# Routing the gathered tokens first, seven places for gathered rows, and one-hot products moved out of PSUM in runs of four tokens

## The chip, the cores and the metric

One Trainium2 chip, one core. The metric is the device time of one execution in microseconds; the median of the runs counts.

## The reference

Two transformer layers over 512 tokens of width 1024, all in float32. Everything of interest is in the last step of the second layer, an expert layer with 16384 experts of one row each:

```python
q = (xn @ wq).reshape(bsz, s, 8, 2, 128)
sub = jnp.einsum('bshpd,hpnd->bshpn', q, subkeys)        # 16 score rows of 128 per token
s_top, i_top = lax.top_k(sub, 16)
cand = s_top[..., 0, :, None] + s_top[..., 1, None, :]   # 16 x 16 per head
best, pos = lax.top_k(cand, 16)
expert = take_along_axis(i_top0 * 128 + i_top1, pos)     # 8 heads x 16 experts per token
gate = softmax(best)
a = gelu(einsum('td,ted->te', x, u_tab[expert]))
y = einsum('te,ted->td', gate * a, v_tab[expert])
```

## The kernel before

**How the experts are computed.** The 512 tokens are four blocks of 128 (tb 0 to 3). For the first 320 tokens (N_U: blocks 0 and 1 and half of block 2) the products with the rows of `u` are made densely: `u_block` takes 128 experts, loads a unit of 512 KB (`raw`, four buffers), splits it in two float32r parts (`whi` by ScalarE, L137, and `wlo` by VectorE, L139), and makes 24 matmuls of 320 columns (three passes times eight), then a gelu. For the first 384 tokens the products with `v` are dense too: `v_block` loads and splits 128 rows of `v` and makes 18 matmuls of 512 columns into six banks that live to the end. The weights between the two come from the routing: `build` makes a matrix of 128 x 128 experts for each token as a product of two one-hot matrices on TensorE (L1048), moves four tokens at a time out of PSUM (ScalarE, L1049), and writes most of it to `g_dram`, some to `gres`.

For the other 192 tokens rows are **gathered**: a gather (L881, an indirect DMA issued by GpSimd) brings one row of 4 KB for each of 128 partitions, 512 KB in all, into one of GBUFS = 4 places, and one VectorE instruction consumes it. There are 64 for the second half of block 2 (`ga2`, L889; two tokens' worth on the two halves of the partitions), then 128 with `u` for block 3 (L897), then 128 with `v` for block 3 (L904, into `h[3]`). A place is free again once VectorE has consumed it.

**Stages.** First 16 projections for the scores, then a *first stage* of 100 `u_block`s whose results go to `a_dram` (the pairs in SPAIR), in which the routing is done alongside; then a *second stage* over 64 pairs of blocks: two `v_block`s for each pair, and for the pairs not in SPAIR also two `u_block`s.

**What sets the order.** Work alongside is written as generators: `route` (`top_keys`, `keys`, `build`) and `gat` (the gathers). Each `yield` gives an assumed number of microseconds, and `advance(gen, us)` lets a generator go on until the allowance is used; a `yield 0.0` ends the call. In the first stage each `u_block` allows R_US = 2.1 for `route` and, once block 2's experts are known (`ready`), G1_US = 0.9 for `gat`, of which a gather takes 1.2; in the second stage each `v_block` allows G_US = 2.4, two gathers. `routed` runs `top_keys` of all blocks, then `keys` 2 and 3, `keys` and `build` of 0 and 1, then whatever of the 64 gathers of block 2 is left in one go (`while not made2: next(gat)`), `weights2`, and `build` of 2. On every engine instructions run in their order; the sequence within that is made by the tile scheduler.

Of the kernel before, what the change touches and what calls it, by code (L numbers as in the profile page):

```python
# [9 lines left out]
F32 = mybir.dt.float32  # L10
# [12 lines left out]
GBUFS = 4  # L23

R_US = 2.1
TOP_US = 4.0
G1_US = 0.9
G_US = 2.4
# [10 lines left out]
N_RES = 2  # L39

# [3 lines left out]
SPILL = [2 * p + j for p in SPAIR for j in range(2)]  # L44
# [15 lines left out]
def tile_layers(ctx: ExitStack, tc: tile.TileContext, A: dict, out: bass.AP):  # L60
# [8 lines left out]
    keep = pool("keep")  # L69
    ring = pool("ring")  # L70
    small = pool("small", bufs=4)
# [778 lines left out]
    gres = []  # L850
# [34 lines left out]
    def gathered():  # L885
        for k in range(64):
            r = gather(A["peer_u"], gidx2, k)
            with tc.issue_after(pace[0]):
                V.scalar_tensor_tensor(r, r, 1.0, hn2, op0=OP.mult, op1=OP.mult, accum_out=ga2[:, k:k + 1])  # L889
            yield 1.2  # L890
        made2.append(True)
        while len(ready) < 2:
            yield 0.0
        for k in range(128):
            r = gather(A["peer_u"], gidx, k)
            with tc.issue_after(pace[0]):
                V.scalar_tensor_tensor(r, r, 1.0, hn3, op0=OP.mult, op1=OP.mult, accum_out=ga[:, k:k + 1])  # L897
            yield 1.2
        S.activation(ga, ga, AF.Gelu_apprx_tanh)
        V.tensor_tensor(ga, ga, ggate, op=OP.mult)  # L900
        for k in range(128):
            r = gather(A["peer_v"], gidx, k)
            with tc.issue_after(pace[0]):
                V.scalar_tensor_tensor(h[3], r, ga[:, k:k + 1], h[3], op0=OP.mult, op1=OP.add)  # L904
            yield 1.2

    def top_keys(sub, tb, hps):
        sv, si = tops[tb]
        for hp in hps:
            x = sub[:, hp, :]  # L910
            with order(pace[0]):
                V.max(out=sv[:, hp, 0:8], in_=x)
                V.max_index(out=si[:, hp, 0:8], in_max=sv[:, hp, 0:8], in_values=x)
                V.match_replace(out=x, in_to_replace=sv[:, hp, 0:8], in_values=x, imm_value=-3.0e38)
                V.max(out=sv[:, hp, 8:16], in_=x)
                V.max_index(out=si[:, hp, 8:16], in_max=sv[:, hp, 8:16], in_values=x)
            yield 1.0

    def keys(pr, tb):
# [15 lines left out]
        for j in range(8):  # L935
# [8 lines left out]
            yield 1.1  # L944
# [18 lines left out]
        for a in range(2):  # L963
            for b0 in range(0, 16, 8):
# [12 lines left out]
                yield 1.2  # L977
# [30 lines left out]
        yield 2.0  # L1008
# [13 lines left out]
    def build(pr, tb):  # L1022

        sT = sTs[tb]
        for ts in range(8):
            gt = pr.tile([128, 128, 16], F32, name="gt", bufs=2)
            for t8 in range(0, 16, 8):
# [15 lines left out]
                for q in range(2):  # L1043
# [15 lines left out]
    with ExitStack() as st:  # L1059
# [20 lines left out]
        sub = [pk.tile([128, 16, 128], F32, name=f"sub{tb}") for tb in range(4)]  # L1080
# [4 lines left out]
        def routed():  # L1085
# [6 lines left out]
            pres = pool("pres", side="right")  # L1092
            gres.extend(pres.tile([128, 24, 8, 16], F32, name=f"gres{g}") for g in range(N_RES))
# [15 lines left out]
        for c4 in range(4):  # L1109
# [25 lines left out]
    with ExitStack() as st:  # L1135
# [45 lines left out]
        for p in range(64):  # L1181
            if p < 63:
# [3 lines left out]
            state["debt"] = advance(gat, state["debt"] + G_US)  # L1186
# [3 lines left out]
            state["debt"] = advance(gat, state["debt"] + G_US)  # L1190
# [139 lines left out]
```

## Time and profile before

| | |
|---|---|
| median of 3 runs | 2220.05 us (2218.74 to 2222.28) |
| the profiled execution | 2223.98 us, span 2222.3 us |
| PE busy | 2082.0 us, 94% of the span |
| VectorE busy | 1583.9 us, 71% |
| ScalarE busy | 863.1 us, 39% |
| gathers | 320, 169.18 MB of 476.47 MB moved |

Reading it: a busy share of TensorE counts matmuls whose ends are modelled, so that 94% is not 94% of what it can do; the pitch between two starts in a full stretch tells more. The clock that was granted to TensorE and the share of the 16 DMA engines stand in the table of stretches. A wait behind an arrow names what ended the idle time before an instruction.

### The profile page before, as it was taken

The numbers are of one execution on the slowest core, as the hardware profiler recorded it, in microseconds if no ns is written. First come the engines' busy times: TensorE is split into PE (matmuls) and PEld (weight loads), VectorE is DVE, ScalarE is ACT, GpSimd is POOL, SyncE is SP. The second block draws the span as 40 slices with busy tenths as digits, with TensorE's granted clock in tenths as the row PEclk, the third lists the DMA queues.
The fourth block names the chain that finished last, engine by engine and source line by source line (L and its number), as shares of the span: only waits on it lengthen the run. The fifth ranks groups of instructions, "written<-read, shape, count | busy, mean of one in ns | idle before, by whom it ended". The sixth has DMA issues, their size and how long they took to land.

```text
span 2222.3 us, 29478 instructions
## 1 busy us (share of the span) xinstructions
PE 2082.0 (94%) x11104; PEld 1767.1 (80%) x11104; DVE 1583.9 (71%) x2880; ACT 863.1 (39%) x1303; POOL 501.1 (23%) x383
## 2 busy tenths in 40 slices
PE   7989999999989999999999998899999899898889
PEld 6737888888777778888999997799787677777777
DVE  6984533332479654569999998887888788778873
ACT  4454422222344433333546765563333233232222
POOL 1000000000001000000031214323555556555550
PEclk9989999999999999999999999899999999999999
DMA  5202333333223213322688999999999999999992
GB/s 190 76 20 76 95 96 100 98 114 95 65 83 100 76 63 101 128 93 77 194 301 291 357 309 338 324 339 373 345 352 351 359 363 370 366 348 363 365 324 95
DMA packets 163281, 476.47 MB, mean 214 GB/s; under 512 B 13865, under 2 KB 57265, under 8 KB 161218
## 3 DMA queue, kind: packets, MB, share of 16 engines
q1 hardware_dynamic: 67104, 259.70, 34.1%
q0 software_dynamic: 46656, 169.18, 20.6%
q10 hardware_dynamic: 49378, 45.71, 6.2%
q8 instruction: 87, 1.43, 0.3%
q14 instruction: 56, 0.46, 0.1%
HBM read 432.18 MB, written 42.09 MB: 213 GB/s over the span
## 4 chain that ended last, share of the span: by engine, by line
PE 40%; issue 25%; DMA 14%; DVE 10%; POOL 9%; ACT 1%; POOLq 0%; DVEq 0%; SPq 0%; ACTq 0%
PE bank_a L155 9%; PE bank_a L156 9%; PE bank_a L157 9%; DMA rows<-in_peer_v_dram,gidx 9%; POOL rows L881 8%; PE bank_b L155 3%; PE bank_b L156 3%; PE bank_b L157 3%; DMA rows<-in_peer_u_dram,gidx 3%; DVE wlo L139 2%; DVE h L904 1%; PE bank_b L1048 1%; DVE rows L889 1%; POOL rstd L163 1%; DMA gl<-g_dram 1%
## 5 line engine op out<-in xcount | busy, mean ns | idle before, releaser
L137 ACT CAST whi<-raw 128x1024 fp32r<-128x1024 f32 (+1 forms) x413 | 432.1, 1047 | 851.1 <-PE bank_a L156 332.7
L139 DVE TENSOR_TENSOR wlo<-raw,whi 128x1024 fp32r<-128x1024 f32 (+1 forms) x413 | 500.4, 1214 | 268.2 <-ACT whi L137 265.9
L155 PE MATMUL bank_a<-xhi,whi 128*128 128x320 f32 (+2 forms) x1600 | 552.8, 346 | 9.4 <-ACT whi L137 8.4
L157 PE MATMUL bank_a<-xhi,wlo 128*128 128x320 f32 (+2 forms) x1600 | 546.9, 342 | 9.6 <-DVE wlo L139 9.6
L156 PE MATMUL bank_a<-xlo,whi 128*128 128x320 f32 (+2 forms) x1600 | 549.8, 344 | 0.6 <-DVE xlo L152 0.6
L881 POOL DMA_INDIRECT rows<-in_peer_u_dram,gidx x192 | 265.9, 1385 | 598.0 <-DVE rows L897 214.0
L155 PEld LDWEIGHTS bank_a<-xhi,whi 128*128 128x128 f32 x1600 | 304.9, 191 | 38.1 <-ACT whi L137 9.2
L157 PEld LDWEIGHTS bank_a<-xhi,wlo 128*128 128x128 f32 x1600 | 305.3, 191 | 36.0 <-DVE wlo L139 10.1
L156 PEld LDWEIGHTS bank_a<-xlo,whi 128*128 128x128 f32 x1600 | 305.8, 191 | 26.9 <-DVE xlo L152 1.6
L155 PE MATMUL bank_a<-whi,wvhi 128*128 128x512 f32 x512 | 209.9, 410 | 46.4 <-ACT wvhi L151 46.4
L881 POOL DMA_INDIRECT rows<-in_peer_v_dram,gidx x128 | 198.9, 1554 | 157.8 <-DVE h L904 136.3
L156 PE MATMUL bank_a<-wlo,wvhi 128*128 128x512 f32 x512 | 208.5, 407 | 3.1 <-DVE wlo L139 3.1
L163 POOL TENSOR_TENSOR rstd<-rstd,neghalf 128x1 f32<-128x1 f32 (+2 forms) x37 | 26.5, 718 | 818.9 <-DVE rstd L162 810.9
L157 PE MATMUL bank_a<-whi,wvlo 128*128 128x512 f32 x512 | 209.1, 408 | 1.5 <-DVE wvlo L152 1.5
L904 DVE SCALAR_TENSOR_TENSOR h<-rows,ga,h 128x1024 f32<-128x1024 f32 x128 | 164.2, 1283 | 60.1 <-DMA rows<-in_peer_v_dram,gidx 59.1
L897 DVE SCALAR_TENSOR_TENSOR rows<-rows,h 128x1024 f32<-128x1024 f32 x128 | 154.8, 1220 | 45.4 <-DMA rows<-in_peer_u_dram,gidx 45.1
L155 PEld LDWEIGHTS bank_a<-whi,wvhi 128*128 128x128 f32 x512 | 101.2, 198 | 70.2 <-ACT wvhi L151 50.7
L157 PEld LDWEIGHTS bank_a<-whi,wvlo 128*128 128x128 f32 x512 | 100.9, 197 | 29.5 <-DVE wvlo L152 8.4
L156 PEld LDWEIGHTS bank_a<-wlo,wvhi 128*128 128x128 f32 x512 | 101.5, 198 | 25.3 <-DVE wlo L139 5.0
L151 ACT CAST wvhi<-gl 128x768 fp32r<-128x768 f32 x56 | 45.6, 831 | 164.8 <-DVE gl L1164 98.1
L1049 ACT ACTIVATE gt<-bank_b 128x512 f32<-128x512 f32 x96 | 96.8, 1119 | 10.8 <-PE bank_b L1048 10.1
L155 PE MATMUL bank_b<-whi,wvhi 128*128 128x512 f32 x256 | 100.7, 393 | 0.0
(391 smaller groups left out, 3364.9 us busy)
## 6 DMA issues: line engine op xcount, KB each, us to landing
raw<-in_wt_dram SPq DMA_DIRECT2D x150, 512.0 KB
raw<-in_ut_dram SPq DMA_DIRECT2D x128, 512.0 KB
raw<-in_peer_v_dram SPq DMA_DIRECT2D x128, 512.0 KB
g_dram<-gt ACTq DMA_DIRECT2D x24, 896.0 KB
gl<-g_dram SPq DMA_DIRECT2D x14, 1536.0 KB
a_dram<-ab ACTq DMA_DIRECT2D x25, 640.0 KB
al<-a_dram SPq DMA_DIRECT2D x25, 640.0 KB
rows<-in_peer_u_dram,gidx POOLq DMA_INDIRECT x192
```

The source lines that it names most:

```text
L137: lead[0] = S.copy(hi[:, :n], raw[:, :n]).ins
L139: pace[0] = V.tensor_tensor(lo[:, :n], raw[:, :n], hi[:, :n].bitcast(F32), op=OP.subtract).ins
L151: a = S.copy(hi, src).ins
L155: T.matmul(o, lh, rh, start=start, stop=False)
L156: T.matmul(o, lh, rl, start=False, stop=False)
L157: T.matmul(o, ll, rh, start=False, stop=stop)
L163: G.tensor_tensor(r, r, neghalf[:, :shape[1]], op=OP.pow)
L881: G.indirect_dma_start(out=r, out_offset=None, in_=table, in_offset=bass.IndirectOffsetOnAxis(ap=idx[:, k:k + 1], axis=0))
L889: V.scalar_tensor_tensor(r, r, 1.0, hn2, op0=OP.mult, op1=OP.mult, accum_out=ga2[:, k:k + 1])
L897: V.scalar_tensor_tensor(r, r, 1.0, hn3, op0=OP.mult, op1=OP.mult, accum_out=ga[:, k:k + 1])
L904: V.scalar_tensor_tensor(h[3], r, ga[:, k:k + 1], h[3], op0=OP.mult, op1=OP.add)
L1049: S.activation(gt[:, :, t8 + 4 * q:t8 + 4 * q + 4].rearrange("p i t -> p t i"), gp, AF.Copy, scale=1.0 if made else 2.0 ** -14)
```

## The change

Six things are changed together.

1. GBUFS goes from 4 to 7. Room for it comes from the descriptor memory of the software DMA queue (`dynamic_dma_scratch_size` set to 4096 bytes a partition) and from `sub[0]` and `sub[1]`, which now lie in the memory of `gres`, allocated earlier for it.
2. Routing order: during the projections only blocks 2 and 3 go through `top_keys`; `keys` 2 and 3 follow; only then `top_keys` of blocks 0 and 1.
3. The assumed times of nearly all steps are others (a step of `top_keys` 1.6 for 1.0, a gather 1.3 for 1.2, a step of `build` 2.7 or 3.4 for 2.4).
4. In the first stage one allowance of 3.6 for each block is shared: 1.0 to the gathers as long as block 2's 64 are not made, then 0.5, and the rest to `route`.
5. In the second stage a `v_block` of a pair in SPAIR allows 2.3, of another pair 3.45.
6. The move out of PSUM writes runs of four tokens: the output is taken as it lies (128 x 4), and the PSUM side is read across.

```diff
-GBUFS = 4
+GBUFS = 7
-R_US = 2.1
-TOP_US = 4.0
-G1_US = 0.9
-G_US = 2.4
+TOP_US = 5.0
+R_US = 3.6
+GATHER = 0.5
+G_US = 2.3
+DMA_SCRATCH = 4096
...
-    gres = []
+    pres = pool("pres", side="right")
+    gres = [pres.tile([128, 24, 8, 16], F32, name=f"gres{g}") for g in range(N_RES)]
...
-                    S.activation(gt[:, :, t8 + 4 * q:t8 + 4 * q + 4].rearrange("p i t -> p t i"), gp, AF.Copy,
+                    S.activation(gt[:, :, t8 + 4 * q:t8 + 4 * q + 4], gp.rearrange("p t i -> p i t"), AF.Copy,
                                  scale=1.0 if made else 2.0 ** -14)
-                yield 2.4
+                yield 3.4 if made else 2.7
...
-        sub = [pk.tile([128, 16, 128], F32, name=f"sub{tb}") for tb in range(4)]
+        sub = [gres[tb].rearrange("p s i t -> p (s i t)")[:, 0:2048].rearrange("p (a n) -> p a n", a=16) if tb < 2 else
+               pk.tile([128, 16, 128], F32, name=f"sub{tb}") for tb in range(4)]
...
             yield from keys(pr, 2)
             yield from keys(pr, 3)
+            for tb in (0, 1):
+                yield from top_keys(sub[tb], tb, range(16))
             for tb in (0, 1):
                 yield from keys(pr, tb)
                 yield from build(pr, tb)
...
-            todo += [top_keys(sub[tb], tb, range(c4 * 4, c4 * 4 + 4)) for tb in (2, 3, 0, 1)]
+            todo += [top_keys(sub[tb], tb, range(c4 * 4, c4 * 4 + 4)) for tb in (2, 3)]
...
-                d1 = advance(route, d1 + R_US)
                 if ready:
-                    d2 = advance(gat, d2 + G1_US)
+                    g1 = GATHER * (2 - len(made2))
+                    d2 = advance(gat, d2 + g1)
+                d1 = advance(route, d1 + R_US - (g1 if ready else 0.0))
...
+            g_us = G_US if p in SPAIR else 1.5 * G_US
...
-            state["debt"] = advance(gat, state["debt"] + G_US)
+            state["debt"] = advance(gat, state["debt"] + g_us)
```

What this moves is best seen on VectorE, which consumes the gathers and makes every `wlo`. In units of 512 KB (counted by `wlo`; the first stage begins behind number 157 and ends behind number 260) the first gather is consumed behind unit 175 before and behind unit 169 now, and 84 gathers stand ahead of unit 261 before, 70 now. Of the 64 steps of `top_keys` 32 stand behind the first stage's beginning before, 48 now.

VectorE around the end of block 2's 64 gathers, before (`rows,ga_6475` is a gather for block 2, `rows,ga` one for block 3, `oh` the one-hot matrices, `wlo` a unit):

```order
L889 SCALAR_TENSOR_TENSOR rows,ga_6475<-rows,h_71 128x1024 x4
L139 TENSOR_TENSOR wlo<-raw,whi 128x1024
L889 SCALAR_TENSOR_TENSOR rows,ga_6475<-rows,h_71 128x1024 x3
L1034 TENSOR_TENSOR oh_12130<-iota_7081,sT_7064 128x1024
L889 SCALAR_TENSOR_TENSOR rows,ga_6475<-rows,h_71 128x1024
L1035 TENSOR_TENSOR oh_12131<-iota_7081,sT_7064 128x1024
L889 SCALAR_TENSOR_TENSOR rows,ga_6475<-rows,h_71 128x1024
L1041 TENSOR_TENSOR ohh<-oh_12131,sT_7064 128x1024
L889 SCALAR_TENSOR_TENSOR rows,ga_6475<-rows,h_71 128x1024 x2
L1041 TENSOR_TENSOR ohl<-oh_12131,sT_7064 128x1024
L889 SCALAR_TENSOR_TENSOR rows,ga_6475<-rows,h_71 128x1024
L139 TENSOR_TENSOR wlo<-raw,whi 128x1024
```

The same place now:

```order
L891 SCALAR_TENSOR_TENSOR rows,ga_6475<-rows,h_71 128x1024
L1037 TENSOR_TENSOR oh_12326<-iota_7086,sT_7068 128x1024
L140 TENSOR_TENSOR wlo<-raw,whi 128x1024
L1036 TENSOR_TENSOR oh_12325<-iota_7086,sT_7068 128x1024
L1043 TENSOR_TENSOR ohh<-oh_12326,sT_7069 128x1024
L1043 TENSOR_TENSOR ohl<-oh_12326,sT_7069 128x1024
L891 SCALAR_TENSOR_TENSOR rows,ga_6475<-rows,h_71 128x1024
L140 TENSOR_TENSOR wlo<-raw,whi 128x1024
L891 SCALAR_TENSOR_TENSOR rows,ga_6475<-rows,h_71 128x1024 x4
L899 SCALAR_TENSOR_TENSOR rows,ga<-rows,h_70 128x1024
```

Before, 18 gathers of block 2 stand between the `wlo` of unit 232 and that of unit 235; now four stand together behind one `wlo`, at unit 243.

VectorE at the end of the program, before (`wvlo` are the split weights, L904 the gathers with `v`, L1200 the final additions):

```order
L904 SCALAR_TENSOR_TENSOR h_73<-rows,ga,h_73 128x1024
L139 TENSOR_TENSOR wlo<-raw,whi 128x1024
L152 TENSOR_TENSOR wvlo<-gl,wvhi 128x24x2x16
L139 TENSOR_TENSOR wlo<-raw,whi 128x1024 x2
L152 TENSOR_TENSOR wvlo<-gl,wvhi 128x24x2x16
L139 TENSOR_TENSOR wlo<-raw,whi 128x1024 x2
L152 TENSOR_TENSOR wvlo<-gl,wvhi 128x24x2x16
L139 TENSOR_TENSOR wlo<-raw,whi 128x1024 x2
L152 TENSOR_TENSOR wvlo<-gl,wvhi 128x24x2x16
L139 TENSOR_TENSOR wlo<-raw,whi 128x1024 x3
L1200 TENSOR_TENSOR h_70<-h_70,bank_a 128x512 x2
```

The same place now:

```order
L140 TENSOR_TENSOR wlo<-raw,whi 128x1024
L906 SCALAR_TENSOR_TENSOR h_73<-rows,ga,h_73 128x1024
L140 TENSOR_TENSOR wlo<-raw,whi 128x1024
L906 SCALAR_TENSOR_TENSOR h_73<-rows,ga,h_73 128x1024 x2
L153 TENSOR_TENSOR wvlo<-gl,wvhi 128x24x2x16
L140 TENSOR_TENSOR wlo<-raw,whi 128x1024
L906 SCALAR_TENSOR_TENSOR h_73<-rows,ga,h_73 128x1024 x2
L140 TENSOR_TENSOR wlo<-raw,whi 128x1024
L906 SCALAR_TENSOR_TENSOR h_73<-rows,ga,h_73 128x1024 x2
L140 TENSOR_TENSOR wlo<-raw,whi 128x1024
L1207 TENSOR_TENSOR h_70<-h_70,bank_a 128x512 x2
```

Before, the last ten units have no gather beside them; now gathers stand between the units up to the last one.

## Rows read from the trace of the kernel before

**Rows 1.** Stretches: microseconds; PE, PEld, DVE, ACT, POOL busy; granted clock; DMA share; GB/s

```profile
960.00:1020.00 60.00, 60.00 (x307) 49.56 (x306) 50.65 (x283) 20.53 (x31) 0.00 (x0) 1.00 0.27 88
1020.00:1210.00 190.00, 179.23 (x1279) 172.46 (x1279) 180.14 (x670) 96.77 (x134) 31.34 (x24) 0.97 0.66 219
1210.00:1350.00 140.00, 139.99 (x1177) 137.21 (x1174) 133.00 (x226) 100.06 (x140) 32.62 (x26) 1.00 0.97 335
1350.00:1420.00 70.00, 48.34 (x346) 45.83 (x345) 56.01 (x92) 30.56 (x44) 29.33 (x24) 0.80 0.94 323
1420.00:1504.00 84.00, 84.00 (x725) 82.71 (x724) 69.84 (x100) 53.64 (x76) 17.76 (x14) 1.00 0.97 336
1504.00:2168.00 664.00, 606.04 (x2758) 506.29 (x2758) 547.77 (x612) 205.00 (x235) 353.75 (x232) 0.95 0.96 357
2168.00:2222.30 54.30, 50.33 (x212) 41.05 (x211) 20.62 (x21) 10.86 (x12) 0.00 (x0) 0.94 0.29 97
```

**Rows 2.** Stretches with line 139 alone (`wlo`): how many units VectorE had begun

```profile
0.00:1020.00 1020.00, 189.06 (x157) 0.99 0.29 93
0.00:1504.00 1504.00, 314.30 (x261) 0.98 0.47 156
0.00:2168.00 2168.00, 488.20 (x403) 0.97 0.62 217
```

**Rows 3.** Burst around 1384 us in order of time: start, length, instruction, idle before, releaser

```profile
1383.97 0.63 PE L157 MATMUL bank_a<-xhi,wlo 128*128 128x320 f32 x1 [9.43 <-DVE wlo L139]
1390.76 1.22 DVE L889 SCALAR_TENSOR_TENSOR rows<-rows,h 128x1024 f32<-128x1024 f32 x1 [2.81 <-DMA rows<-in_peer_u_dram,gidx]
```

**Rows 4.** Groups by line, 1504 to 2168 us: count, busy us, mean ns, idle before, releasers

```profile
L881 POOL DMA_INDIRECT rows<-in_peer_v_dram,gidx x128 | 198.9, 1554 | 157.8 <-DVE h L904 136.3 <-DMA rows<-in_peer_v_dram,gidx 9.6 <-issue 4.9
L155 PE MATMUL bank_a<-whi,wvhi 128*128 128x512 f32 x466 | 191.5, 411 | 46.4 <-ACT wvhi L151 46.4
L904 DVE SCALAR_TENSOR_TENSOR h<-rows,ga,h 128x1024 f32<-128x1024 f32 x128 | 164.2, 1283 | 60.1 <-DMA rows<-in_peer_v_dram,gidx 59.1
L897 DVE SCALAR_TENSOR_TENSOR rows<-rows,h 128x1024 f32<-128x1024 f32 x108 | 130.4, 1221 | 44.5 <-DMA rows<-in_peer_u_dram,gidx 44.2
```

**Rows 5.** A pair not in SPAIR around 2099 us, in order of time, VectorE, ScalarE, TensorE

```profile
2093.89 1.28 DVE L904 SCALAR_TENSOR_TENSOR h<-rows,ga,h 128x1024 f32<-128x1024 f32 x1 [2.26 <-DMA rows<-in_peer_v_dram,gidx]
2098.70 1.56 ACT L151 CAST wvhi<-gl 128x768 fp32r<-128x768 f32 x2 [10.84 <-DVE gl L1164]
2099.58 0.80 PE L155 MATMUL bank_a<-whi,wvhi 128*128 128x512 f32 x1 [6.88 <-ACT wvhi L151]
```

**Rows 6.** Groups by line and shape, 940 to 1535 us: VectorE and ScalarE

```profile
L889 DVE SCALAR_TENSOR_TENSOR rows<-rows,h 128x1024 f32<-128x1024 f32 x64 | 77.7, 1219 | 15.3 <-DMA rows<-in_peer_u_dram,gidx 15.3
L916 DVE FIND_INDEX8 si<-sv,sub 128x8 uint32<-128x128 f32 x64 | 17.8, 286 | 0.0
L1049 ACT ACTIVATE gt<-bank_b 128x512 f32<-128x512 f32 x96 | 96.8, 1119 | 10.8 <-PE bank_b L1048 10.1
L1121 ACT COPY sub<-bank_b 128x512 f32<-128x512 f32 x16 | 8.2, 601 | 2.3 <-PE bank_b L1116 2.3
```

**Rows 7.** DMA: the gathers' queue (packets, MB, share of 16 engines), then two short stretches

```profile
q0 software_dynamic: 46656, 169.18, 20.6%
1525.00:1550.00 25.00, 25.00 (x137) 22.48 (x136) 18.84 (x28) 8.94 (x12) 9.52 (x6) 1.00 1.02 414
2075.00:2100.00 25.00, 18.12 (x92) 15.51 (x91) 19.48 (x19) 5.11 (x7) 11.16 (x8) 0.95 1.01 396
```

**Rows 8.** TensorE in full stretches: two neighbours in a `u_block` and in a `v_block`

```profile
1470.43 0.31 PE L155 MATMUL bank_a<-xhi,whi 128*128 128x320 f32 x1
1470.58 0.31 PE L156 MATMUL bank_a<-xlo,whi 128*128 128x320 f32 x1
...
2185.07 0.39 PE L156 MATMUL bank_b<-wlo,wvhi 128*128 128x512 f32 x1
2185.30 0.39 PE L157 MATMUL bank_b<-whi,wvlo 128*128 128x512 f32 x1
```

More of the change, by code (lines that the diff above doesn't have):

```diff
@@ L39 @@
 N_RES = 2
+DMA_SCRATCH = 4096
 N_U = 320
 SPAIR = [N_HEAD + i for i in range(64 - N_HEAD) if i * NSPILL // 2 // (64 - N_HEAD) != (i + 1) * NSPILL // 2 // (64 - N_HEAD)]
-SPILL = [2 * p + j for p in SPAIR for j in range(2)]
 MAGIC = 1.5 * 2.0 ** 23
@@ L69, in tile_layers @@
     keep = pool("keep")
+    small = pool("small", bufs=4)
     ring = pool("ring")
-    small = pool("small", bufs=4)
     ps = pool("ps", bufs=4, space=PSUM)
@@ L889, in gathered @@
                 V.scalar_tensor_tensor(r, r, 1.0, hn2, op0=OP.mult, op1=OP.mult, accum_out=ga2[:, k:k + 1])
-            yield 1.2
+            yield 1.3
         made2.append(True)
@@ L897, in gathered @@
                 V.scalar_tensor_tensor(r, r, 1.0, hn3, op0=OP.mult, op1=OP.mult, accum_out=ga[:, k:k + 1])
-            yield 1.2
+            yield 1.3
         S.activation(ga, ga, AF.Gelu_apprx_tanh)
@@ L904, in gathered @@
                 V.scalar_tensor_tensor(h[3], r, ga[:, k:k + 1], h[3], op0=OP.mult, op1=OP.add)
-            yield 1.2
+            yield 1.3
     def top_keys(sub, tb, hps):
@@ L916, in top_keys @@
                 V.max_index(out=si[:, hp, 8:16], in_max=sv[:, hp, 8:16], in_values=x)
-            yield 1.0
+            yield 1.6
     def keys(pr, tb):
@@ L943, in keys @@
             V.max_index(out=bp[:, j, 8:16], in_max=o8, in_values=x)
-            yield 1.1
+            yield 1.4
         ki_ = pr.tile([128, 2, 128], U32, name="ki_")
@@ L976, in keys @@
                         T.matmul(pt2[:, a * 128:(a + 1) * 128], turn16, e3[:, b], start=(b0 + b == 0), stop=(b0 + b == 15))
-                yield 1.2
+                yield 1.4
         if tb == 2:
@@ L1007, in keys @@
             S.activation(gT2, pt[:, 320:384], AF.Copy, scale=2.0 ** -14)
-        yield 2.0
+        yield 3.0
     def weights2():
@@ L1091, in routed @@
             st2.close()
-            pres = pool("pres", side="right")
-            gres.extend(pres.tile([128, 24, 8, 16], F32, name=f"gres{g}") for g in range(N_RES))
             pr = pool("pr", stack=st)
@@ L1121, in tile_layers @@
                 S.copy(sub[tb][:, c4 * 4:c4 * 4 + 4, :], sb_[tb].rearrange("p (a n) -> p a n", a=4))
-            todo += [top_keys(sub[tb], tb, range(c4 * 4, c4 * 4 + 4)) for tb in (2, 3, 0, 1)]
+            todo += [top_keys(sub[tb], tb, range(c4 * 4, c4 * 4 + 4)) for tb in (2, 3)]
         keyed.append(True)
-        for n4 in range(0, len(SPILL), 4):
+        for n4 in range(0, 2 * len(SPAIR), 4):
             ab = ptop.tile([128, 4, N_U], F32, name="ab", bufs=2)
             for j in range(4):
-                u_block(SPILL[n4 + j], ab[:, j, :], "a")
-                d1 = advance(route, d1 + R_US)
+                u_block(2 * SPAIR[(n4 + j) // 2] + j % 2, ab[:, j, :], "a")
                 if ready:
-                    d2 = advance(gat, d2 + G1_US)
+                    g1 = GATHER * (2 - len(made2))
+                    d2 = advance(gat, d2 + g1)
+                d1 = advance(route, d1 + R_US - (g1 if ready else 0.0))
             nc.scalar.dma_start(a_dram[n4 // 4], ab)
@@ L1189, in tile_layers @@
             v_block(2 * p + 1, w)
-            state["debt"] = advance(gat, state["debt"] + G_US)
+            state["debt"] = advance(gat, state["debt"] + g_us)
             w = wn
```

2 lines of the change are left out of this document (1 added, 1 removed).

## Prediction, made before the changed kernel ran

> **What bounds the kernel now.** I read the table of stretches first, because the busy shares of the whole program mix stages. The change touches nothing that matters ahead of 1020 us: there TensorE is full, with the DMA engines at 0.27 [rows 1]. From 1020 us, where unit 157 is due [rows 2], there are three parts.
>
> The first stage, 1020 to 1504 us, has 104 units in 484 us. VectorE is busy for 180 + 133 + 56 + 70 = 439 us of it, and in the undisturbed stretch of 1210 to 1350 us for 133 of 140 us, 95% [rows 1]. VectorE is what this stage waits for, TensorE being close behind. One hole stands out: from 1350 to 1420 us TensorE is busy for 48 of 70 us at a granted clock of 0.80. It belongs to the remaining 18 gathers of block 2, made in one go: TensorE idles 9.43 us for a `wlo` that stands behind them, and VectorE itself waits up to 2.81 us for rows, with only four places ahead [rows 3].
>
> The second stage up to the last gather, 1504 to 2168 us, has 236 gathers consumed (108 + 128) [rows 4] in 664 us, one in 2.81 us. No engine is full: VectorE 548, TensorE 606 of 664 at clock 0.95. The DMA engines are, with 0.96 [rows 1]. The waits say how this reaches TensorE. GpSimd waits 136 us for VectorE to free a place, VectorE waits 59 + 44 = 103 us for rows [rows 4]: a ring of four places, each gone round in about 11 us. And while VectorE waits, what stands behind it waits: around 2099 us the weights of a pair with its own `u_block`s are 10.84 us late for ScalarE and TensorE idles 6.88 us [rows 5]; there are ten such gaps, 46 us in all [rows 4].
>
> The end, from 2168 us: no gathers, DMA at 0.29, and TensorE works off the last blocks at its own pace [rows 1].
>
> **The change part by part.** *First stage, VectorE.* Sixteen steps of `top_keys` move into it (48 for 32), five searches of 0.286 us each, 16 x 1.4 = 22 us [rows 6]. Fourteen gathers leave it (70 for 84), 14 x 1.22 = 17 us. So its work is 439 + 5 = 444 us. The burst is gone but for four gathers in a row, and with seven places those have landed when they are wanted; so I let VectorE run at the 95% that it reaches in the undisturbed stretch: 444 / 0.95 = 467 us, end of the stage at 1487 for 1504. What could stand in the way is TensorE: 104 blocks of 24 matmuls at a pitch of 0.145 us [rows 8] are 362 us, and the one-hot products are 832 short ones; below 467 us together. The bounds for this term: 1475 if VectorE runs at 98%, 1509 if it keeps the 439 of 484 us of before (91%: 444 / 0.91 = 488).
>
> *The memory for it* (smaller descriptor memory, `sub` in `gres`) I cost at nothing: `gres` is written by `build` only, which stands behind `top_keys` of blocks 0 and 1 on VectorE anyway. The trace doesn't show how many descriptors wait; a lack of room would bring the pace of the second stage back to that of before, and that case is a rival below.
>
> *The move out of PSUM.* 96 instructions of 1.119 us; the same 512 elements written in one run take 0.601 us [rows 6]. The write was one element in 64 bytes and becomes runs of 16 bytes, but the read, which was in one run, now goes across. Bounds: 96 x 0.52 = 50 us saved on ScalarE, or 50 us more if the read costs once more what the write did. The Trainium skill, "SBUF — State Buffer", section "Door 1: The DMA port swizzle", speaks of lines of 16 bytes in SBUF and of 8 bytes in PSUM, with a penalty for each new line; by it the write gets free and the read is penalised, and the gain could vanish. I take half the gain, 25 us. On the path it is nothing either way: ScalarE is busy for 97 + 100 + 31 + 54 = 281 of 484 us in the first stage [rows 1], and 281 + 50 would still be below VectorE's 444.
>
> *Second stage, DMA.* The engines' time in it is 0.96 x 664 + 0.29 x 54 = 653 us. A gather takes 20.6% of 2222 / 320 = 1.43 us of all engines [rows 7], so the 14 more make it 673. Before, the last 54 us used little of it; now the gathers reach to the last unit, and only the last 18 us (three blocks of TensorE, the additions, the stores) carry some 5 us of DMA. The rest, 668 us, runs at a share between the 0.96 of before and the full 1.0 which short stretches show [rows 7]. With seven places more transfers are queued at any time, so I take the middle, 0.98: 668 / 0.98 + 18 = 700 us. Seven places let a row be 7 x 2.8 = 20 us on its way instead of 11, so VectorE's 103 us of waiting go, and what is late next is the DMA itself. VectorE has 548 + 21 + 14 x 1.28 = 587 us of work in those 700.
>
> *Second stage, TensorE.* 466 matmuls on four of six banks are 116 `v_block`s, 2097 matmuls of the 2758; the others are `u_block`s. At the pitches of 0.23 and 0.145 us [rows 8] that is 482 + 96 = 578 us, and 49 more behind 2168 us: 627 us, so hidden by 700. The unequal allowance (3.45 beside pairs with `u_block`s, 2.3 beside the others) moves gathers to where TensorE has more to do; I give it no price of its own, since with the DMA as the bound only the sum counts.
>
> Sum: 1487 + 700 = 2187 us of span. The median of the runs lies 2.2 us below the span of the profiled execution (2220.05 against 2222.3), so **2185 us**, 1.6% faster. With the share at 0.96 or 1.0 it is 2199 or 2171.
>
> **The rivals.** *The DMA has room* (chance 0.20). Short stretches moved 414 and 396 GB/s, the stage 357 [rows 1, 7]. If the deeper queue holds that rate, TensorE is the bound: 627 us, half of the 46 us of gaps, 7 us of additions and stores, 657 in all: 1487 + 657 - 2 = 2142. Against it: the share stood at 0.96 already. The Trainium skill, "DMA: Bandwidth & Descriptors", section "Specifications", gives some 358 GB/s as HBM's limit for a core, and by that rule this rival is impossible; the row with 414 GB/s speaks against the rule as a cap here. As a mechanism: 0.357 x 664 + 0.097 x 54 = 242 MB, with 14 x 0.53 MB more 250 MB, at 357 GB/s 700 us, and the 18 us of the end: 1487 + 718 - 2 = 2203. This is my forecast's slow edge, and I count it there.
>
> *The places do nothing* (0.17): rows land no sooner because the DMA engines are shared, or because the smaller descriptor memory lets no more than four be on the way, and a gather keeps its 2.81 us: 250 x 2.81 + 18 = 721 us, 1487 + 721 - 2 = 2206.
>
> *Slower* (0.13): the same unchanged pace, and the first stage doesn't shorten. The place is VectorE behind unit 157: the new allowance is 3.6 us of routing and gathers on top of 1.22 us for a `wlo`, 4.82 for each of 100 blocks, 482 us, where the trace of before shows 484 for 104 units in spite of the hole. Then the stage ends at 1509, and 1509 + 721 - 2 = 2228, 0.4% slower. It decides from a pace of 2.78 us on: below that the second stage makes good what the first loses. For it: the 14 gathers went from a stage that had room on the DMA engines early (0.66 up to 1210 us) to the one that is full. Against it: the allowances add up durations of single instructions, and instructions overlap; the busy time is what counts.
>
> **How the numbers follow.** Forecast 0.50 (2165 to 2205), room on the DMA 0.20 (2142), useless places 0.17 (2206), slower 0.13 (2228). The range of eight in ten reaches from 2146, a little above the case with room, to 2222, just short of the slow case. Faster by over 0.2% (below 2215.6; about what a measurement of this kernel can tell from no change): all but a little of the first three, 0.78. Within 0.2%: 0.10. Slower by more: 0.12.
>
> **What would show it.** The hole near 1380 us gone, with no stretch of the first stage at a clock below 0.9, and unit 260 done near 1487 us. VectorE's waits for rows down from 103 us in the second stage to below 40. The DMA share at 0.97 or more up to the last 20 us, and a gather every 2.7 to 2.8 us. The gaps of TensorE in pairs with `u_block`s at about half. The eviction of four tokens between 0.6 and 1.1 us. I am wrong if rows still arrive late with seven places (then the engines or the descriptors are the limit), or if unit 260 is later than 1504 us, or if TensorE becomes full in the second stage (then the DMA had room).

## The result, and the profile after

| | before | after |
|---|---|---|
| median of 4 runs each, same chip | 2219.39 us | 2136.15 us (2130.1 to 2137.3) |
| ratio after to before | | 0.9622, 95% interval 0.9596 to 0.9649 |
| the profiled execution, span | 2222.3 us | 2128.4 us |
| last gather consumed | 2168 us | 2111 us |

The changed kernel is 3.8% faster. I had said 2185 us, in a range from 2146 up: it came out below the range, beside the rival that I gave 0.20 (room on the DMA, 2142 us). The profiled execution of the changed kernel is its fastest one, 6 us below the median.

Table of stretches of the changed kernel, columns as in [rows 1]: length; busy time of PE, PEld, DVE, ACT, POOL; granted clock; DMA share; GB/s.

```profile
1020.00:1210.00 190.00, 180.98 (x1207) 171.67 (x1206) 173.26 (x730) 83.33 (x117) 38.69 (x32) 0.99 0.67 234
1210.00:1350.00 140.00, 135.28 (x1120) 131.42 (x1119) 136.93 (x277) 79.08 (x132) 31.48 (x25) 0.99 0.92 317
1350.00:1420.00 70.00, 70.00 (x610) 68.67 (x609) 69.89 (x108) 40.78 (x77) 20.65 (x16) 1.00 0.99 342
1350.00:1484.00 134.00, 132.47 (x1211) 129.29 (x1210) 131.03 (x198) 77.23 (x149) 25.36 (x20) 1.00 0.98 334
1484.00:2111.00 627.00, 614.01 (x2912) 519.97 (x2911) 572.99 (x652) 217.09 (x247) 392.30 (x243) 0.99 1.00 393
2111.00:2128.40 17.40, 13.50 (x60) 10.86 (x58) 5.72 (x8) 0.00 (x0) 0.00 (x0) 0.99 0.32 121
```

How many `wlo` VectorE had begun (line 140 alone):

```profile
0.00:1484.00 1484.00, 315.45 (x261) 0.99 0.46 154
0.00:2111.00 2111.00, 498.92 (x412) 0.99 0.62 225
```

Unit 261, begun by 1504 us before [rows 2], is begun by 1484 now, and the hole of [rows 3] is gone: 1350 to 1420 us is full at clock 1.00 (48 of 70 us at 0.80 before [rows 1]). The second stage takes 250 gathers in 627 us, one in 2.51 us for 2.81, and the DMA engines move 393 GB/s in it for 357 [rows 1]. The first stage gave 20 us, the second, from 1484 us to the end, takes 644 us where 700 were forecast.

Groups of the changed kernel in the second stage: count, busy us, mean ns, idle time before them, what ended it.

```profile
L883 POOL DMA_INDIRECT rows<-in_peer_v_dram,gidx x128 | 207.0, 1617 | 115.2 <-DVE h L906 90.3 <-DVE rows L899 12.3 <-issue 7.0
L156 PE MATMUL bank_a<-whi,wvhi 128*128 128x512 f32 x512 | 201.1, 393 | 8.2 <-ACT wvhi L152 8.1
L906 DVE SCALAR_TENSOR_TENSOR h<-rows,ga,h 128x1024 f32<-128x1024 f32 x128 | 164.3, 1284 | 5.2 <-DMA rows<-in_peer_v_dram,gidx 4.2
L899 DVE SCALAR_TENSOR_TENSOR rows<-rows,h 128x1024 f32<-128x1024 f32 x122 | 145.4, 1220 | 7.7 <-DMA rows<-in_peer_u_dram,gidx 7.7
L1170 DVE TENSOR_TENSOR gl<-al,gl 128x640 f32<-128x640 f32 x46 | 36.4, 819 | 25.7 <-DMA al<-a_dram 20.1 <-DMA gl<-g_dram 5.6
```

VectorE's 103 us of waiting for rows [rows 4] are 12, TensorE's 46 us of gaps before `wvhi` are 8. TensorE is now busy for 614 of 627 us at clock 0.99, where it had 606 of 664 at 0.95. What VectorE waits for most is a load that the prediction did not mention: `al`, the first stage's results (20.1 us in five waits). One of these waits, in order of time, with what stands behind it:

```profile
1840.92 0.33 SPq L1153 DMA_DIRECT2D al<-a_dram  x1
...
1845.42 1.56 DVE L1170 TENSOR_TENSOR gl<-al,gl 128x640 f32<-128x640 f32 x2 [2.20 <-DMA gl<-g_dram]
1847.01 0.33 SPq L1153 DMA_DIRECT2D al<-a_dram  x1
1853.34 0.82 DVE L1170 TENSOR_TENSOR gl<-al,gl 128x640 f32<-128x640 f32 x1 [4.03 <-DMA al<-a_dram]
1863.47 1.57 ACT L152 CAST wvhi<-gl 128x768 fp32r<-128x768 f32 x2 [6.11 <-DVE gl L1170]
1864.35 0.50 PE L156 MATMUL bank_a<-whi,wvhi 128*128 128x512 f32 x1 [3.62 <-ACT wvhi L152]
```

A load of `al` is issued when the last product with its buffer is made: the one at 1847.01 stands right behind the two products in a row of 1845.42. The next product wants the load before it, issued at 1840.92, and starts 12.4 us later; for the last 4.03 us VectorE stands. What is queued behind it, another product and its weights, comes late in turn, and eleven microseconds later TensorE idles 3.62 us. In the kernel before there were three such waits, 8.0 us together:

```profile
DVE gl L1164 <- DMA al<-a_dram: 8.0, 3, 4.8
```

Such a line gives the waiting instruction, what it waits for, the total in us, the number of waits and the longest one.

### The profile page after: what moved, and what is told of

Its sections match the earlier page's. It is cut to its first block, busy times and chain, and to the rows that moved or that the text cites. A ratio compares the mean times of both kernels' runs of the same rounds, so it can differ in the third digit from the quotient of the medians.

```text
span 2128.4 us, 29432 instructions
## 1 busy us (share of the span) xinstructions
PE 2048.3 (96%) x11104; PEld 1743.5 (82%) x11104; DVE 1575.3 (74%) x2880; ACT 821.0 (39%) x1303; POOL 524.3 (25%) x383
## 3 DMA queue, kind: packets, MB, share of 16 engines
q1 hardware_dynamic: 67104, 259.70, 34.4%
q0 software_dynamic: 46656, 169.18, 20.8%
q8 instruction: 87, 1.43, 0.3%
## 4 chain that ended last, share of the span: by engine, by line
PE 25%; DVE 18%; issue 14%; DMA 10%; POOL 3%; ACT 1%; DVEq 0%; POOLq 0%; SPq 0%; ACTq 0%
PE bank_a L158 5%; PE bank_a L156 5%; PE bank_a L157 5%; DVE wlo L140 5%; DMA rows<-in_peer_u_dram,gidx 3%; POOL rows L883 3%; DMA rows<-in_peer_v_dram,gidx 3%; DVE rows L899 2%; DMA al<-a_dram 2%; PE bank_b L156 2%; PE bank_b L157 2%; PE bank_b L158 2%; DVE rows L891 2%; PE bank_b L1050 1%; DMA raw<-in_ut_dram 1%
## 5 line engine op out<-in xcount | busy, mean ns | idle before, releaser
L883 POOL DMA_INDIRECT rows<-in_peer_u_dram,gidx x192 | 280.9, 1463 | 554.2 <-DVE gidx L984 145.0
L883 POOL DMA_INDIRECT rows<-in_peer_v_dram,gidx x128 | 207.0, 1617 | 115.2 <-DVE h L906 90.3
L156 PE MATMUL bank_a<-whi,wvhi 128*128 128x512 f32 x512 | 201.1, 393 | 8.2 <-ACT wvhi L152 8.1
L158 PE MATMUL bank_a<-whi,wvlo 128*128 128x512 f32 x512 | 201.4, 393 | 1.9 <-DVE wvlo L153 1.9
L157 PE MATMUL bank_a<-wlo,wvhi 128*128 128x512 f32 x512 | 200.6, 392 | 2.4 <-DVE wlo L140 2.4
L156 PEld LDWEIGHTS bank_a<-whi,wvhi 128*128 128x128 f32 x512 | 96.9, 189 | 29.1 <-ACT wvhi L152 10.2
L157 PEld LDWEIGHTS bank_a<-wlo,wvhi 128*128 128x128 f32 x512 | 96.8, 189 | 22.4 <-DVE wlo L140 3.2
L157 PE MATMUL bank_b<-wlo,wvhi 128*128 128x512 f32 x256 | 99.6, 389 | 0.0
L158 PE MATMUL bank_b<-whi,wvlo 128*128 128x512 f32 x256 | 99.6, 389 | 0.0
```

The costliest lines, as they stand in the source:

```text
L156: T.matmul(o, lh, rh, start=start, stop=False)
L157: T.matmul(o, lh, rl, start=False, stop=False)
L158: T.matmul(o, ll, rh, start=False, stop=stop)
L883: G.indirect_dma_start(out=r, out_offset=None, in_=table, in_offset=bass.IndirectOffsetOnAxis(ap=idx[:, k:k + 1], axis=0))
```

## Experiments

### The parts of the change, one by one

**The new order with four places.**

```diff
-GBUFS = 7
+GBUFS = 4
```

> The changed kernel with four places for rows instead of seven, all else kept. Theory 'places': the second stage was slow because a place is only free again after VectorE has consumed it, so four places hold too few transfers in the queue; a gather goes back to about 2.8 us, 250 of them and the end are some 720 us behind a first stage that ends near 1485 us: about 2200 us, VectorE's waits for rows near 100 us again. Rival 'order': the gain comes from the new order and the spread gathers, and stays without the places: below 2150 us.

Measured 2202.89 us, ratio 0.9922 (0.9891 to 0.9953). Unit 261 comes at 1490 us, the last gather at 2187.5: 250 gathers in 697 us, 2.79 us each. Its stretch in the middle of the second stage, columns as above:

```profile
1600.00:1900.00 300.00, 272.06 (x1218) 225.06 (x1219) 241.97 (x310) 92.07 (x103) 155.93 (x105) 0.96 0.96 359
```

This is the kernel of my rival "the places do nothing" (2206 us), and it comes to that time: the first stage's gain stays, the second stage keeps the old pace. VectorE waits 55 + 48 = 103 us for rows, as before:

```profile
DVE rows L899 <- DMA rows<-in_peer_u_dram,gidx: 54.5, 41, 5.4
DVE h L906 <- DMA rows<-in_peer_v_dram,gidx: 48.2, 36, 3.9
```

**The kernel before with seven places.** The smaller descriptor memory goes with it, to make the room.

```diff
-GBUFS = 4
+GBUFS = 7
...
-    nc = _bacc.Bacc("TRN2", target_bir_lowering=False, num_devices=1)
+    nc = _bacc.Bacc("TRN2", target_bir_lowering=False, num_devices=1, dynamic_dma_scratch_size=4096)
```

> The kernel before with seven places (and the descriptor memory at 4096 bytes that makes room for them), old order and old move. Theory 'places': the second stage gets as fast as in the changed kernel, 645 to 655 us from unit 261 on, and the hole near 1380 us shrinks by some of its 20 us: 2140 to 2160 us. Rival 'order': 2200 us or more.

Measured 2142.33 us, ratio 0.9649 (0.9622 to 0.9676). 236 gathers in 591 us, 2.51 us each, and 12 us of waits for rows. The hole stays, with a DMA share of 1.00 in it:

```profile
1350.00:1420.00 70.00, 51.64 (x395) 49.25 (x395) 62.10 (x101) 34.83 (x50) 34.53 (x25) 0.85 1.00 351
```

So the places, with the memory for them, are worth 76 us in the kernel before, all the other parts without them 16, and everything together 83.

**Seven places for units in place of rows**, in the kernel before: `raw` gets seven buffers, rows keep four. The smaller descriptor memory goes with it here too.

```diff
-        raw = ring.tile([128, 1024], F32, tag="raw", name="raw", bufs=4)
+        raw = ring.tile([128, 1024], F32, tag="raw", name="raw", bufs=7)
...
-    nc = _bacc.Bacc("TRN2", target_bir_lowering=False, num_devices=1)
+    nc = _bacc.Bacc("TRN2", target_bir_lowering=False, num_devices=1, dynamic_dma_scratch_size=4096)
```

> The kernel before with seven buffers for raw units instead of four, and still four places for rows. Theory 'places': VectorE goes on waiting about 100 us for rows in the second stage, time 2200 to 2225 us. Rival 'any queue': whatever is in flight more lifts the DMA rate from 357 towards 390 GB/s, and the time falls to 2150 to 2180 us.

Measured 2213.49 us, ratio 0.9982 (0.9964 to 1.0). VectorE waits 54.5 + 51.2 us for rows as before, and the rate doesn't rise:

```profile
1600.00:1900.00 300.00, 273.78 (x1206) 226.22 (x1206) 243.09 (x302) 90.21 (x103) 160.66 (x107) 0.94 0.95 354
```

ScalarE's waits for units, 106 us from 1490 us on in the kernel before, are gone, and the time hardly moves. More places are of no use as such; they have to be those of the transfers that hold the pace.

**The smaller descriptor memory alone**, in the kernel before.

```diff
+    nc = _bacc.Bacc("TRN2", target_bir_lowering=False, num_devices=1, dynamic_dma_scratch_size=4096)
```

> The kernel before with the smaller descriptor memory alone (4096 bytes a partition), still four places. The prediction costed this memory at nothing. If that is right, 2214 to 2224 us as before, DMA share 0.96 and 357 GB/s in the second stage, 100 us of waits for rows. If the room for descriptors mattered, GpSimd's gathers would take longer to issue (1554 ns before) and the time would be 2230 or more; if it were a part of the gain, below 2205.

Measured 2218.9 us, ratio 1.0009 (0.9993 to 1.0025): nothing, as costed.

**The old move out of PSUM**, in the changed kernel.

```diff
-                    S.activation(gt[:, :, t8 + 4 * q:t8 + 4 * q + 4], gp.rearrange("p t i -> p i t"), AF.Copy,
+                    S.activation(gt[:, :, t8 + 4 * q:t8 + 4 * q + 4].rearrange("p i t -> p t i"), gp, AF.Copy,
```

> The changed kernel with the old move out of PSUM (writes 64 bytes apart, reads in one run). Theory 'off the path': ScalarE gets 50 us of work more in the first stage and has room for it, 2131 to 2145 us. Rival 'on the path': the faster move shortened what VectorE and TensorE wait for, 10 to 30 us more than the changed kernel.

Measured 2131.99 us, ratio 0.9602 (0.9575 to 0.9629), no different from the changed kernel. The move in the changed kernel, and with the old one:

```profile
L1051 ACT ACTIVATE gt<-bank_b 128x512 f32<-128x512 f32 x96 | 52.4, 598 | 14.8 <-PE bank_b L1050 10.0 <-DMA g_dram<-gt 4.0
```

```profile
L1051 ACT ACTIVATE gt<-bank_b 128x512 f32<-128x512 f32 x96 | 97.1, 1121 | 10.7 <-DMA g_dram<-gt 5.2 <-PE bank_b L1050 4.8
```

ScalarE saves 96 x 0.523 = 50 us, all that the better bound gave, and the time doesn't move, since ScalarE is not waited for there.

**The same allowance for all pairs**, in the changed kernel.

```diff
-            g_us = G_US if p in SPAIR else 1.5 * G_US
+            g_us = 2.6
```

> The changed kernel with one allowance of 2.6 us (two gathers) for each block of the second stage, in place of 2.3 beside pairs in SPAIR and 3.45 beside the others. The prediction gave the unequal allowance no price. If that was right also with TensorE as the bound, 2130 to 2142 us. If the unequal one is needed (a pair without u_blocks takes TensorE less time, so that two gathers beside each of its blocks come faster than the DMA engines bring them), TensorE shows gaps again beside pairs in SPAIR, wvhi gaps of 20 us or more for 8, and the time is 2148 or more.

Measured 2133.02 us, ratio 0.9619 (0.9599 to 0.9639). TensorE's gaps before the split weights `wvhi` grow from 8.1 to 11.5 us, which the time doesn't show:

```profile
PE bank_a L156 <- ACT wvhi L152: 11.5, 5, 4.9
```

### How many places

Five and six places in the changed kernel; the instructions of VectorE and SyncE stand in the same order as with seven.

```diff
-GBUFS = 7
+GBUFS = 5
```

> The changed kernel with five places for rows. It stands at 2136 us with seven places (250 gathers in 627 us, 2.51 each) and at 2203 with four (2.79 each). Theory A (a ring of four goes round in 11.2 us, because a row is that long on its way, and each place more shortens the pace until TensorE is full): a ring of five that still goes round in 11.2 us would allow 2.24 us a gather, faster than TensorE lets the stage go (2.51), so 2136 to 2150 us, VectorE's waits for rows below 30 us in the second stage (12 with seven places, 95 with four). Theory B (the rows come back later the more of them are on their way, since all share the DMA engines; the gain rises place by place): the pace lies a third of the way between, 2.70 us, 1490 + 250 x 2.70 + 18 = 2183, waits for rows 50 to 75 us.

```diff
-GBUFS = 7
+GBUFS = 6
```

> The changed kernel with six places for rows. Four gave 2203 us, five 2160, seven 2136. If the gain comes place by place until the DMA engines or TensorE are full, the sixth gives what is left between five and seven in greater part: 2138 to 2148 us, waits for rows 20 to 30 us (47 with five, 12 with seven). If seven are still short, 2148 to 2152, half way.

Measured 2160.26 us (0.9736, 0.972 to 0.9752) and 2139.29 us (0.9642, 0.9615 to 0.967). Columns of all these rows as above; five places, six, and seven:

```profile
1600.00:1900.00 300.00, 284.73 (x1299) 235.90 (x1298) 260.77 (x325) 97.27 (x109) 175.38 (x114) 0.98 1.00 382
```

```profile
1600.00:1900.00 300.00, 286.44 (x1322) 239.77 (x1321) 264.69 (x325) 98.52 (x111) 181.96 (x116) 0.99 1.00 391
```

```profile
1600.00:1900.00 300.00, 289.92 (x1346) 242.81 (x1345) 268.90 (x329) 100.36 (x113) 186.63 (x116) 0.99 1.01 399
```

VectorE's waits for rows, five places, then six:

```profile
DVE rows L899 <- DMA rows<-in_peer_u_dram,gidx: 24.8, 26, 4.5
DVE h L906 <- DMA rows<-in_peer_v_dram,gidx: 22.2, 16, 3.6
```

```profile
DVE rows L899 <- DMA rows<-in_peer_u_dram,gidx: 16.6, 21, 2.0
DVE h L906 <- DMA rows<-in_peer_v_dram,gidx: 7.5, 11, 1.5
```

With the row of four places above: 359, 382, 391, 399 GB/s, waits for rows 103, 47, 24, 12 us, time 2203, 2160, 2139, 2136. The waits halve with each place. The ring of four doesn't simply speed up by a place's share: with five it would go at 11.2 / 5 = 2.24 us, faster than TensorE lets it, and the time would have been 2136 to 2150. A row is longer on its way when more are on theirs: from issue to landing the medians with `u` and `v` are 8.3 and 9.0 us with five places, 10.6 and 10.5 with six, and 10.9 and 13.1 with seven and one allowance for all pairs. My other theory, a third of the gain with the fifth place (2183 us), was too low: the fifth place alone brings 43 of the 67 us. The waits for `al` grow meanwhile: 10.0, 16.2, 18.4 and 20.1 us with four, five, six and seven places.

### What holds the second stage now

**Eight more blocks in the first stage**, since TensorE seemed to be the bound of the second.

```diff
-R_US = 3.6
+R_US = 3.35
-G_US = 2.3
-NSPILL = 100
+G_US = 2.45
+NSPILL = 108
```

> The changed kernel with 108 u_blocks in the first stage for 100 (eight fewer in the second), R_US 3.35 for 3.6 and G_US 2.45 for 2.3. If TensorE is what the second stage waits for now and VectorE what the first waits for, eight u_blocks of 24 matmuls at 0.145 us, 28 us of TensorE, leave the stage that is full and cost the first stage eight wlo of 1.22 us on VectorE (10 us) and 3.5 us of TensorE each where TensorE has room: 2115 to 2130 us. If the DMA engines are the bound of the second stage at 393 GB/s (share 1.00), the eight units take 4 MB, 10 us, off it and the first stage gives 10 to 25 us back: 2134 to 2150.

Measured 2154.37 us, ratio 0.9709 (0.9693 to 0.9726): slower than the changed kernel by 18 us, and more than either theory gave. The eight units lengthen the first stage by 26 us (unit 269 by 1510 us, for 261 by 1484), where TensorE and VectorE were both at 97% or more already from 1210 us on. The second, from there to the end, takes 643 us for 644: TensorE has less to do, but VectorE still waits 18 us for `al`, and for rows 26 where it was 12. Both allowances changed along with the eight units, so the 18 us are not put down to one cause:

```profile
1510.00:2120.00 610.00, 583.99 (x2704) 488.17 (x2704) 555.99 (x640) 203.97 (x231) 380.53 (x243) 0.98 1.00 397
```

**Less work for TensorE**, in the changed kernel and in the kernel before: the pass with the second part of `v` is left out of every `v_block`, 6 of 18 matmuls.

```diff
-                    mm3(yb_[tb][hf], ...)
+                    T.matmul(yb_[tb][hf], w[0][...], vu[0][...], start=i1 == 0, stop=False)
+                    T.matmul(yb_[tb][hf], w[1][...], vu[0][...], start=False, stop=i1 == 127)
```

> The changed kernel with two of the three passes of each v_block: the pass with the second part of v is left out (its split is still made), 6 of 18 matmuls, 128 x 6 x 0.23 = 177 us of TensorE less in the second stage; DMA, VectorE and ScalarE keep their work. Theory A (with seven places TensorE alone holds the second stage, 614 of 627 us): the stage falls to what comes next, VectorE's 573 us of work at 97%, 590 us, or the 246 MB at the 410 GB/s of the short stretches, 600 us: 2095 to 2110 us. Theory B (the DMA engines hold it already at the 393 to 401 GB/s that the stage shows): 246 MB at 401 are 614 us, so 2120 us or more, whatever TensorE has to do.

> The kernel before (four places) with the same pass left out, 177 us of TensorE less in the second stage. If four places alone hold the pace of the gathers (2.81 us each, a ring that goes round in 11.2 us), they keep 2.7 to 2.8 us and the kernel gains the end only (54 us without gathers, a third of its TensorE work): 2170 to 2205 us, TensorE idle for a quarter of the second stage, DMA share still 0.96 at 360 GB/s. If TensorE held the pace together with the rows, the gathers come below 2.6 us each and the time falls below 2150.

Measured 2173.63 us (0.9802, 0.9781 to 0.9823) with seven places, 37 us **slower** than with all three passes, and 2191.19 us (0.9889, 0.9862 to 0.9916) with four. The first, then a group of it in the second stage:

```profile
1600.00:1900.00 300.00, 228.58 (x938) 182.89 (x937) 254.07 (x319) 98.01 (x109) 175.72 (x112) 0.88 0.97 378
```

```profile
L138 ACT CAST whi<-raw 128x1024 fp32r<-128x1024 f32 x151 | 158.5, 1049 | 384.1 <-DMA raw<-in_peer_v_dram 298.7 <-DMA raw<-in_ut_dram 48.3 <-DVE gl L1170 11.1
```

The pair is inconclusive. The scheduler, with shorter blocks to place, put the instructions of VectorE and SyncE in another order; no wait for rows is left among VectorE's waits, but ScalarE waits 299 us for units of `v` (110 in the changed kernel), and TensorE, idle for a quarter of the time, is granted 0.88. By these waits the run with seven places is held by another ring, that of the units, which no run tests; so it says nothing on what held the changed kernel. The run with four places fell where a ring of four was expected to put it, with 366 GB/s, but its order is another too, and it waits as long for units.

**One load of `al` for the whole second stage.** TensorE, ScalarE and GpSimd keep their order.

```diff
-                    if n % 2 == 0:
+                    if n == 0:
                         state["al"] = pv.tile([128, 4, N_U], F32, name="al", bufs=2)
```

> The changed kernel with one load of the first stage's results for the whole second stage, used for all pairs (the other 24 loads of 655 KB are left out, 15.7 MB, 38 us of the DMA engines at 410 GB/s); TensorE, VectorE and ScalarE keep their work. If the DMA engines hold the second stage, it falls until TensorE is full: 13 us of idle time are left to TensorE in it, so 2120 to 2128 us. If TensorE alone holds it, 2131 to 2138 as with seven places. If it comes out below 2118, neither was full.

Measured 2113.1 us, ratio 0.9532 (0.9511 to 0.9553).

```profile
1600.00:1900.00 300.00, 300.00 (x1425) 255.63 (x1424) 282.37 (x339) 107.00 (x120) 195.33 (x124) 1.00 1.01 394
```

TensorE is full at clock 1.00, without a recorded wait from 1490 us to the end, and the stage from 1484 us takes 625 us, close to my 627 for TensorE. With these loads gone, the gathers come at the pace that TensorE sets. The time is below 2118, so by the last sentence of the expectation neither TensorE nor the DMA engines were full in the changed kernel. I had taken TensorE's busy 614 us for its work; a matmul behind a gap is counted longer (0.50 us in the row at 1864.35, where the mean is 0.39). Counted from start to start, the matmuls of the changed kernel that come later than their pitch lose 19 us from 1490 us on, and 0.1 us here.

**Every second load of `al`, or all of them with half the bytes.**

```diff
-                    if n % 2 == 0:
+                    if n % 4 == 0:
```

> The changed kernel with every second load of the first stage's results (12 of 25 are left out, 7.9 MB, 20 us of the DMA engines at 400 GB/s; TensorE's, ScalarE's and the gathers' order stay as they are). If the bytes hold the second stage, half the dose gives half or more of the 23 us that the whole gave: 2116 to 2125 us, TensorE idle for less than 6 us between 1600 and 1900 (10 with all loads, none with one load). If the gain came from the waits of SyncE's queue behind these loads rather than from bytes, it is not proportional: 2128 or more, since every second wait stays.

```diff
-    a_dram = drp.tile([32, 128, 4, N_U], F32, name="a_dram")
+    a_dram = drp.tile([32, 128, 4, N_U], F16, name="a_dram")
...
-            ab = ptop.tile([128, 4, N_U], F32, name="ab", bufs=2)
+            ab = ptop.tile([128, 4, N_U], F16, name="ab", bufs=2)
...
-                        state["al"] = pv.tile([128, 4, N_U], F32, name="al", bufs=2)
+                        state["al"] = pv.tile([128, 4, N_U], F16, name="al", bufs=2)
```

> The changed kernel with the first stage's results kept in 16-bit floats on their way through the memory (ab, a_dram, al), 327 KB for 655 each way. With all 24 later loads left out the kernel came to 2113 us, so the second stage is held by the DMA engines until TensorE is full. If that is so here too, half of that traffic gives half to most of that gain: 2116 to 2126 us, and the first stage, with 8 MB less to write, is unchanged or a few us shorter. If the mixed types slow VectorE's product (822 ns for 640 elements), or another order of the instructions costs more than the traffic gives, 2130 or more.

Measured 2115.82 us (0.9536, 0.9514 to 0.9558) and 2133.33 us (0.9607, 0.9589 to 0.9625). Half the loads took away about as much as all; half the bytes, in a somewhat other order of instructions, took nothing that shows. The first, the second, and the second's wait (us, times, longest):

```profile
1600.00:1900.00 300.00, 300.00 (x1424) 255.14 (x1424) 282.37 (x341) 106.01 (x119) 194.95 (x124) 1.00 1.02 406
```

```profile
1600.00:1900.00 300.00, 289.43 (x1340) 242.97 (x1339) 268.30 (x332) 100.40 (x112) 186.78 (x119) 0.99 0.99 383
```

```profile
DVE gl L1170 <- DMA al<-a_dram: 26.5, 5, 7.5
```

So it isn't the bytes in the first place. With half the loads no wait for `al` is left at all (I had expected every second one to stay); in 16 bits VectorE still waits 26.5 us, as each load is still issued only when one of two buffers comes free.

**A third buffer for `al`, and four in 16 bits.** The first changes no other line, and the order on TensorE, ScalarE and GpSimd stays. On VectorE a few products with `al`, and in two places the gathers and units around them, come earlier or later than in the changed kernel, just as in the runs with one load and with every second one.

```diff
-                        state["al"] = pv.tile([128, 4, N_U], F32, name="al", bufs=2)
+                        state["al"] = pv.tile([128, 4, N_U], F32, name="al", bufs=3)
```

> The changed kernel with three buffers for the first stage's results (al) in place of two; the bytes are the same, the order on TensorE and ScalarE too. In the changed kernel VectorE waits 20 us in five places for an al that was asked for only when its buffer came free, some 9 us before. If these waits are what the run with one load took away, 2112 to 2120 us, VectorE's waits for al gone, DMA above 400 GB/s between 1600 and 1900 us, TensorE there without a gap. If the bytes of these loads hold the stage, 2130 to 2138 as with two buffers, other waits coming in their place.

```diff
-                        state["al"] = pv.tile([128, 4, N_U], F16, name="al", bufs=2)
+                        state["al"] = pv.tile([128, 4, N_U], F16, name="al", bufs=4)
```

> The kernel with the first stage's results in 16-bit floats, four buffers for them in place of two. With two it took 2133 us in spite of 8 MB less, and VectorE waited 26 us for them. If the waits are the cause, 2112 to 2120 us here; if the bytes and the waits both count, 2105 to 2112; if neither, 2130 or more.

Measured 2125.02 us (0.959, 0.9571 to 0.9609) and 2117.4 us (0.955, 0.9531 to 0.9568). The first with its wait for `al`, then the second:

```profile
1600.00:1900.00 300.00, 296.89 (x1400) 251.74 (x1399) 274.69 (x336) 103.50 (x116) 192.92 (x121) 0.99 1.02 410
```

```profile
DVE gl L1170 <- DMA al<-a_dram: 1.8, 1, 1.8
```

```profile
1600.00:1900.00 300.00, 300.00 (x1425) 255.51 (x1424) 282.22 (x342) 105.75 (x119) 196.62 (x124) 1.00 1.02 405
```

What shows the waits' price is the pair in 16 bits: the same bytes and the same order on all compute engines, two buffers against four, 2133 against 2117 us. With four buffers no wait for `al` is left, and TensorE is full, as with the loads left out.

In 32 bits a third buffer takes the waits from 20.1 to 1.8 us, with all bytes still moved, 410 GB/s over 300 us. All its times (2121.8 to 2129.5 us) lie below those of the changed kernel (2130.1 to 2137.3), but the intervals of the ratios touch, so the 11 us between the medians are not sure. Its 2125 us lies between the two ranges that I had given.

The bytes seem to count for something too. The runs with three buffers, with every second load and with one load have the same order on VectorE, ScalarE, GpSimd and TensorE, and come to 2125, 2116 and 2113 us; the first interval (0.9571 to 0.9609) lies clear of the other two (at most 0.9558). How much of these 9 to 12 us are bytes, and how much the 1.8 us and other waits that are left, no run parts.

## Why the prediction was wrong

**First stage: right.** 444 us of VectorE at 95% gave 1487; the rows give 173 + 137 + 131 = 441 us in 464 (95%), and 1484. The burst went as described. (The bound for 98% should have read 1473, as 444 / 0.98 = 453; nothing hangs on it.)

**Descriptor memory, unequal allowance, move: nothing on the path, right.** The move's size was at the better bound (598 ns), not half way. The Trainium skill, "SBUF — State Buffer", section "Door 1: The DMA port swizzle", says of its lines of 8 bytes in PSUM that access out of sequence slows matmuls. I had carried that over to ScalarE's read and halved the gain; the read across PSUM showed no penalty in these 96 instructions.

**Second stage, DMA: the step that failed.** I took the DMA engines for what bounds the second stage, read their share of 0.96 as that of a resource that is full, and took 1.43 us of all engines for a gather as a constant: 653 + 20 = 673 us of engine time, so 700 us. The bytes were right (0.393 x 627 + 0.121 x 17.4 = 248 MB for 250), the engine time for them was not: 627 x 1.00 + 17.4 x 0.32 = 633 us. A share of 0.96 with four places went with 359 GB/s, 1.00 to 1.02 with seven went with 399 to 410. Four kernels that differ in the number of places alone show the rate as a result of how many rows may be on their way. With four places the ring of rows held the stage, and the 359 GB/s were no limit of the engines.

**What comes late next.** Waits for rows below 40 us: right, 12. TensorE's gaps in pairs with `u_block`s at about half: they fell further, from 46 to 8 us. "What is late next is the DMA itself": wrong. It is TensorE, whose 627 us I had worked out and put aside as hidden by 700 (625 for the whole stage where nothing interrupts it), with the waits for `al` on top, which grew from 8.0 us in the kernel before to 20.1. The whole from 1484 us on is 644 us.

**The rival.** "The DMA has room" had the mechanism and, with 657 us for the stage, a time 6 us from the median. That closeness is partly luck: the stage took 644 us in the profile, and the median lies 7.8 us above the profile's span, where I had put it 2.2 below. I gave it 0.20 because of that 0.96, against two rows of 414 and 396 GB/s [rows 7] that spoke for it. The page that I weighed there, the Trainium skill, "DMA: Bandwidth & Descriptors", section "Specifications", with 358 GB/s for a core, sat just where four places had put the rate; the runs with 399 and 410 GB/s over 300 us stand against it as a cap here. The "places do nothing" rival was refuted by undoing the places alone (2203 us), the "slower" one by the first stage.

## What to carry to other kernels

A DMA share near 1 at a steady rate is not yet a limit: if short stretches of the same kernel move more, and a consumer waits for a ring with few places, give that ring places and read the rate again. Add places one by one to see where it flattens, and look for the next load with few buffers to become the late one; here a 4 us wait on VectorE came out as a gap on TensorE eleven microseconds later. When an experiment takes work away, compare the order of the instructions before reading its time. An engine's floor that you worked out and put aside as hidden can be the next bound, as it was here, and belongs in the range.

## What the runs showed of the hardware

**The same packets took less of the engines' time with more places for rows.** The two large queues move the same 169.18 and 259.70 MB before and after. The units' queue before, then both after:

```profile
q1 hardware_dynamic: 67104, 259.70, 34.1%
```

```profile
q1 hardware_dynamic: 67104, 259.70, 34.4%
q0 software_dynamic: 46656, 169.18, 20.8%
```

Before they took 20.6 [rows 7] and 34.1% of 2222.3 us, 1216 us together; after, 55.2% of 2128.4 us, 1175 us. The changed kernel with four places took 1222, with five 1202, with six 1186. So the busy share of the engines is no measure of the bytes that they could still move.

**Reading PSUM across cost ScalarE nothing, writing SBUF across cost it double.** 598 ns with the read at a stride and runs of 16 bytes written, 1121 ns with the read in one run and one element in 64 bytes written, 601 ns with both in one run, in another instruction of ScalarE [rows 6].

**Taking work from TensorE made the kernel slower** (2174 for 2136 us), in another order of instructions and at a granted clock of 0.88 for 0.99 in the same stretch. I can't part the two.
